# Moving two of eight convolution blocks behind the first attention, and one block off GpSimd

## The chip, the cores and the metric

One core of a Trainium2 chip runs the whole program. The metric is the device time of one execution in microseconds (us); several executions are timed and their median is given. The engines are called as in the profile: PE is TensorE (matrix products), DVE is VectorE, ACT is ScalarE, POOL is GpSimd, SP issues the DMA transfers.

## The reference, cut to what matters

The program is a transformer block of a convolution branch, an attention branch and a feed-forward part, followed by two more attention layers. Sequence length is 512, model width 1024, batch 1, all in float32. The change touches the first block alone:

```python
h = rms_norm(x, norm1_g[l])
z = h @ w_in[l]
glu_in, q, k, v, gate_logits = jnp.split(z, SPLITS, axis=-1)
a_val, a_gate = jnp.split(glu_in, 2, axis=-1)
a = a_val * jax.nn.sigmoid(a_gate)
a = causal_depthwise_conv(a, conv_w[l], conv_b[l])      # 1024 channels, 31 taps each
a = jax.nn.silu(rms_norm(a, conv_norm_g[l]))            # the norm sums over all 1024 channels
y_a = a @ w_conv_out[l]
...                                                     # attention of 16 heads on q, k, v -> o
y_b = o @ w_attn_out[l]
g_a, g_b = jnp.split(jax.nn.sigmoid(gate_logits + gate_b[l]), 2, axis=-1)
x = x + (g_a * y_a + g_b * y_b) @ w_out[l]
```

The depthwise convolution needs only `a`, so it can run at any time between the first input products and the norm behind it. That norm needs all 1024 channels.

## The kernel before

All activations lie with channels on the 128 partitions and the 512 positions along the row, so 1024 channels are eight blocks c = 0 to 7. Each float32 product is made of three matmuls on split operands (high part times high part, lines 301 to 303). A step of a product over 128 input channels is called a chunk here: three matmuls of 512 columns. One output block of 128 channels is eight chunks. The weights of a block are loaded by SP into `wraw` (two buffers), copied to `whi` by ACT (line 119), and the rest `wlo` is made by POOL (line 123); a `wraw` buffer is free for the next transfer only when POOL has made its `wlo`.

PE's order is written out by hand: products go into a list (`pe`), and `pe.pull(n)` emits n chunks. After every chunk a function `beside` can emit other work. The bank of PSUM that a product is written to comes from two banks (`pj`), or from four (`pj` and `s`) where `banks["wide"]` is set. Inside the stage "glu" the orders of PE, DVE, ACT and POOL are those of the code. From the first attention on only PE's is; the planner orders the other engines, by the place in the code and by when it expects an operand.

The stages around the change, in the order of the code:

1. "glu", first half: for each c the products of gate and value (16 products, 128 chunks); line 883 on DVE makes `a` of block c and appends the block to a waiting list. From the ninth chunk on, `beside` emits convolution taps: each chunk earns `PACES` credits, 1.03 taps for DVE and 0.26 for POOL.
2. "glu", second half: eight products of the gates of the first branch (64 chunks), taps still beside them.
3. "loop1": 44 chunks (`LEAD[0]`) of q, k and v for the first two pairs of heads with their norms (lines 918 to 932), taps now at 0.6 and 0.24 per chunk; then `taps("dve", 1000)` emits what is left of DVE's taps; then the attention over eight pairs of heads with further products between its steps. Its transposes go to the three PSUM banks `pt` (line 593), from which ACT and DVE take them (lines 595 and 596).
4. "mid1": five gate products (40 chunks), the sum of squares over the convolved blocks (lines 1010 to 1014), the products with `w_attn_out` (64 chunks). After `YB` = 28 of these 64 chunks PE sums over the channels (`pn`), ACT makes `rc` of it, and DVE and ACT make the operands `aS` of `w_conv_out` from the eight blocks (lines 1036 to 1042). Then come the products with `w_conv_out`, block 0 and 1 side by side. Line 1022 on DVE empties the bank of each `w_attn_out` product.

A block of the convolution is 30 taps and a first multiplication (line 824, ACT). On DVE a tap is one instruction (line 831) that adds into a `pt` bank, which ACT copies out at the end (line 833). Two blocks (three towards the end of one) are taken in turn, so that neighbouring taps belong to different blocks where two are there. On POOL (blocks 1 and 3, `ON_POOL`) a tap is two instructions: ACT multiplies into one of four buffers (line 836), POOL adds (line 837). So DVE has 6 x 30 = 180 taps and POOL 2 x 30 = 60.

Of the kernel before, what the change touches and what calls it, by code (L numbers as in the profile page):

```python
# [32 lines left out]
LN_EPS = 1e-5  # L33
OFF = (0, 128, 384, 768)
LEAD = (44, 34, 38)
ON_POOL = (1, 3)
PACES = {"dve": (1.03, 0.6), "pool": (0.26, 0.24)}
YB = 28
PIECES = 4
GATES3 = ((3, 3), (3, 3), (3, 4), (4, 5), (5, 5), (5, 6), (6, 6), (6, 8))  # L40
P6 = (1, 1, 1, 0, 1, 1, 0, 0, 1, 0)
# [107 lines left out]
def model_kernel(ctx: ExitStack, tc: tile.TileContext, x, norm1_g, w_in, gate_b, conv_w, conv_b, conv_norm_g,  # L149
# [21 lines left out]
    def ps_t():  # L171
        return ps("pt", 3)
# [17 lines left out]
    def act(o, i, func, **kw):  # L190

        ins = nc.scalar.activation(o, i, func, **kw).ins  # L192
        if ordered["load"] is not None and hT:
            tc.add_manual_dep(ins, ordered["load"].name, no_sync)
        ordered["since"].append(ins)

    def act_tables(name):
        ordered["load"], since = None, ordered["since"] or ordered["before"]
        ordered["since"], ordered["before"] = [], since
        if name is not None:  # L200
            ordered["load"] = nc.scalar.preload_act_table_set(name).ins
            for ins in since:
                tc.add_manual_dep(ordered["load"], ins.name, no_sync)
# [191 lines left out]
    def kept():  # L395
        return keep.tile([128, S], F32, name="S8", bufs=ND)
# [26 lines left out]
    with tc.tile_pool(name="rows", bufs=1) as rows, tc.manual_schedule(engines={  # L423
# [21 lines left out]
        for r in range(2):  # L445
            a = slice(64 * r, 64 * r + 64)
# [35 lines left out]
    def columns():  # L482
        p = ps_t()
        for c in range(ND):
            nc.tensor.transpose(p[:, CW * c:CW * c + CW], cr[c // 4][:, 128 * (c % 4):128 * (c % 4) + 128], ident[:CW, :CW])
        nc.vector.tensor_scalar(cw.rearrange("p a b -> p (a b)"), p[:, :ND * CW], 0.5, None, op0=OP.mult)
        p = ps_t()
        nc.tensor.transpose(p[:, :NV], vr, ident[:NV, :NV])
        nc.vector.tensor_copy(vec, p[:, :NV])
        nc.vector.tensor_scalar(gate_half, vec[:, 0:16], 0.5, None, op0=OP.mult)  # L490
        nc.vector.tensor_scalar(cg_half, vec[:, 24:32], 0.5, None, op0=OP.mult)
        nc.vector.tensor_scalar(qg8, vec[:, 56:57], 0.125, None, op0=OP.mult)
        p = ps_t()
        for j in range(2):
            nc.tensor.transpose(p[:, 88 * j:88 * j + 88], fr[:, j, :], ident[:88, :88])
        pv = p[:, :176].rearrange("p (a b) -> p a b", a=4)
        nc.vector.tensor_copy(fw[:, :, :NF], pv[:, :, :NF])
        nc.vector.tensor_scalar(fw[:, :, NF:], pv[:, :, NF:], 0.5, None, op0=OP.mult)

    def tmp(pool):  # L500
        return pool.tile([128, S], F32, name="tmp", bufs={"dsa": 5, "loop1": 5, "loop3": 2, "glu": 3}[pool.name])
# [284 lines left out]
    with tc.tile_pool(name="mix1", bufs=1) as mix1:  # L786
# [20 lines left out]

        o32 = mix1.tile([128, ND, S], F32, name="o32")
        accs, tga = [], {}
        waiting = {"dve": [], "pool": []}  # L810
        lanes = {"dve": [], "pool": []}
        credit = {"dve": 0.0, "pool": 0.0}
        pace = {}
# [25 lines left out]
        def taps(who, n):  # L839

            on, wait = lanes[who], waiting[who]
            while n >= 1:
                while wait and (len(on) < 2 or (len(on) == 2 and min(t.left for t in on) < 4)):
                    on.append(Conv(*wait.pop(0)))
                if not on:
                    break
                t = on.pop(0)
                t.tap()
                if t.left:
                    on.insert(min(1, len(on)), t)  # L850
                n -= 1
            return n
# [11 lines left out]
        def gate_a(c, t):  # L864
            return Product(w_in, 0, 8, 5120 + 128 * c, hT, gate_done(c, t))

        with tc.tile_pool(name="glu", bufs=1) as gp, tc.manual_schedule(engines={
                mybir.EngineType.PE, mybir.EngineType.DVE, mybir.EngineType.Activation, mybir.EngineType.Pool}):
            act_tables("exp_and_others")
            banks["wide"] = True  # L870

            def glu(c):
                t = tmp(gp)

                def gate(p):
                    act(t, p, AF.Tanh, scale=0.5)

                def val(p):
                    def out():
                        accs.append(kept())  # L880
                        on_pool = c in ON_POOL
                        a = o32[:, ND - 1 - ON_POOL.index(c), :] if on_pool else accs[c]
                        nc.vector.scalar_tensor_tensor(a, t, 1.0, p, op0=OP.add, op1=OP.mult)
                        credit["dve"] -= 1
                        waiting["pool" if on_pool else "dve"].append((c, a))
                    pe.after(3, out)

                return (Product(w_in, 0, 8, 1024 + 128 * c, hT, gate), Product(w_in, 0, 8, 128 * c, hT, val))

            for c in range(ND):  # L890
                for pr in glu(c):
                    pe.skewed(pr)
                if c == 0:
                    pe.pull(8)
                    columns()
                    pace.update({who: p[0] for who, p in PACES.items()})
                    pe.beside = beside
                pe.pull(len(pe.todo))
            for c in range(ND):
                t = mix1.tile([128, S], F32, name="tg", bufs=ND - 1) if c < ND - 1 else rc2  # L900
                pe.skewed(gate_a(c, t))
                pe.pull(len(pe.todo))
            pe.finish()
            pace.update({who: p[1] for who, p in PACES.items()})

# [89 lines left out]
        act_tables(None)  # L995
        with tc.tile_pool(name="mid1", bufs=1) as mp:
            banks["wide"] = True
            oS = []
            for c in range(ND):
                h, l = act_pair(mp, "C", ND)  # L1000
# [19 lines left out]
            def yb_done(c):  # L1020
                t = tga[ND + c]
                return lambda p: nc.vector.scalar_tensor_tensor(t, t, 1.0, p, op0=OP.add, op1=OP.mult)

            for c in range(ND):
                pe.add(w_attn_out, 0, 8, 128 * c, oS, yb_done(c))
            pe.pull(YB)
            pn = ps_t()
# [138 lines left out]
    gs, og, waiting = {}, [], {}  # L1166
# [419 lines left out]
```

## Time and profile before

| | us |
|---|---|
| timed runs, median of 3 (lowest to highest) | 1601.13 (1597.56 to 1601.93) |
| the profiled execution, timed | 1601.03 |
| its span in the profile | 1598.9 |

In the profile PE is busy 1527.2 us of the span, DVE 1121.4, ACT 845.4, POOL 806.5. The granted clock of PE is given as a share of its upper level, 2.4 GHz; the lower level, 1.2 GHz, is 0.5. Times in the text are from the span's start. A row of a timeline gives start and length in us, and in brackets how long the engine stood idle before it and whose work ended that.

### The profile page before, as it was taken

What the parts mean: (1) busy time and instruction counts of PE and PEld (TensorE: products, weight loads), DVE (VectorE), ACT (ScalarE), POOL (GpSimd) and SP (SyncE); (2) the same over time, 40 slices, a digit from 0 to 9 for tenths busy, and PEclk for the clock granted to TensorE, in tenths of its full rate; (3) what the DMA queues carried; (4) which work ended last, traced back from release to release, by engine and by line L of the source; (5) the groups of instructions that cost most, each with busy time, mean ns of one, the idle gap of its engine ahead of it and who ended that gap; (6) DMA issues with size and microseconds to landing.
All of it is one profiled execution on the core that took longest, in us unless ns stands there. A gap on an engine that the chain in (4) does not pass through costs nothing.

```text
span 1598.9 us, 21378 instructions
## 1 busy us (share of the span) xinstructions
PE 1527.2 (96%) x7870; PEld 1296.7 (81%) x7870; DVE 1121.4 (70%) x1837; ACT 845.4 (53%) x1524; POOL 806.5 (50%) x680
## 2 busy tenths in 40 slices
PE   7999799998999999999999999999999789999996
PEld 6877688887878888888888887888887678888885
DVE  8998777776166467727735669988887765777764
ACT  4455787777552444424333444366766345666652
POOL 3789944332744653454444474445442875334324
PEclk9999899999999999999999999999999899999998
DMA  4323212221233423343333242322220313212212
GB/s 149 88 87 98 86 54 73 60 67 40 67 105 105 126 86 92 93 118 91 90 110 89 84 125 66 80 80 66 67 67 14 92 40 106 67 54 80 67 52 80
DMA packets 234604, 130.37 MB, mean 82 GB/s; under 512 B 5206, under 2 KB 232774, under 8 KB 234500
## 3 DMA queue, kind: packets, MB, share of 16 engines
q1 hardware_dynamic: 234356, 128.75, 27.7%
q8 instruction: 62, 1.02, 0.3%
q14 instruction: 42, 0.34, 0.1%
q10 hardware_dynamic: 144, 0.26, 0.0%
HBM read 126.90 MB, written 2.10 MB: 81 GB/s over the span
## 4 chain that ended last, share of the span: by engine, by line
PE 57%; DVE 23%; ACT 7%; POOL 5%; issue 5%; DMA 2%; DVEq 0%; SPq 0%; ACTq 0%; POOLq 0%
PE pj L301 10%; PE pj L302 9%; PE pj L303 9%; PE s L302 5%; PE s L303 5%; PE s L301 5%; DVE pt L831 5%; PE o L512 2%; POOL wlo L123 2%; PE pt L593 2%; PE pj L325 2%; PE pj L327 2%; PE pj L326 2%; POOL S L837 2%; DVE score L1442 1%
## 5 line engine op out<-in xcount | busy, mean ns | idle before, releaser
L123 POOL TENSOR_TENSOR wlo<-wraw,whi 128x256 fp32r<-128x256 f32 (+2 forms) x548 | 653.8, 1218 | 684.4 <-ACT whi L119 639.0
L301 PE MATMUL pj<-Ah,whi 128*128 128x512 f32 (+3 forms) x896 | 362.2, 404 | 15.2 <-DVE v L718 9.8
L119 ACT CAST whi<-wraw 128x1024 fp32r<-128x1024 f32 (+3 forms) x255 | 243.8, 965 | 224.3 <-PE pj L302 82.1
L303 PE MATMUL pj<-Ah,wlo 128*128 128x512 f32 (+3 forms) x896 | 350.4, 391 | 2.5 <-POOL wlo L123 2.5
L302 PE MATMUL pj<-Al,whi 128*128 128x512 f32 (+3 forms) x896 | 350.7, 391 | 0.0
L301 PEld LDWEIGHTS pj<-Ah,whi 128*128 128x128 f32 (+1 forms) x896 | 171.2, 191 | 41.9 <-issue 9.1
L303 PEld LDWEIGHTS pj<-Ah,wlo 128*128 128x128 f32 (+1 forms) x896 | 170.3, 190 | 39.1 <-POOL wlo L123 3.4
L302 PEld LDWEIGHTS pj<-Al,whi 128*128 128x128 f32 (+1 forms) x896 | 171.1, 191 | 24.4
L301 PE MATMUL s<-Ah,whi 128*128 128x512 f32 (+1 forms) x352 | 135.8, 386 | 4.0 <-ACT Ah L1298 4.0
L302 PE MATMUL s<-Al,whi 128*128 128x512 f32 (+1 forms) x352 | 135.7, 386 | 3.6 <-DVE Al L1299 3.6
L303 PE MATMUL s<-Ah,wlo 128*128 128x512 f32 (+1 forms) x352 | 135.6, 385 | 1.0 <-POOL wlo L123 1.0
L831 DVE SCALAR_TENSOR_TENSOR pt<-S,cw,pt 128x496 f32<-128x496 f32 (+19 forms) x180 | 124.8, 738 | 6.4 <-ACT pt L824 3.8
L325 PE MATMUL pj<-whi,Ah 128*128 128x256 f32 x384 | 112.4, 293 | 1.4 <-DVE q L533 1.4
L596 DVE TENSOR_TENSOR PTl<-pt,PTh 128x512 fp32r<-128x512 f32 x144 | 86.0, 598 | 32.9 <-ACT PTh L595 31.9
L327 PE MATMUL pj<-whi,Al 128*128 128x256 f32 x384 | 108.4, 282 | 0.0
L326 PE MATMUL pj<-wlo,Ah 128*128 128x256 f32 x384 | 108.3, 282 | 0.0
L192 ACT ACTIVATE P<-P,nm 128x128 f32<-128x128 f32 (+3 forms) x128 | 72.0, 563 | 63.2 <-DVE nm L626 61.9
L744 DVE SCALAR_TENSOR_TENSOR u<-ur,fw,u 128x511 f32<-128x511 f32 x44 | 74.9, 1705 | 37.5 <-ACT u L743 37.5
L837 POOL TENSOR_TENSOR S<-S,o 128x511 f32<-128x511 f32 (+29 forms) x60 | 78.2, 1317 | 15.4 <-ACT o L836 14.3
L595 ACT CAST PTh<-pt 128x512 fp32r<-128x512 f32 x144 | 73.1, 513 | 19.6 <-PE pt L593 19.1
L302 PEld LDWEIGHTS s<-Al,whi 128*128 128x128 f32 x352 | 67.8, 193 | 17.1 <-DVE Al L1299 4.5
L301 PEld LDWEIGHTS s<-Ah,whi 128*128 128x128 f32 x352 | 67.9, 193 | 17.1 <-ACT Ah L1298 4.6
(334 smaller groups left out, 3250.8 us busy)
## 6 DMA issues: line engine op xcount, KB each, us to landing
wraw<-in_w_in_dram SPq DMA_DIRECT2D x56, 512.0 KB
wraw<-in_w_up_dram SPq DMA_DIRECT2D x44, 512.0 KB
wraw<-in_w_in_a_dram SPq DMA_DIRECT2D x36, 512.0 KB
wraw<-in_w_in_b_dram SPq DMA_DIRECT2D x32, 512.0 KB
wraw<-in_w_down_dram SPq DMA_DIRECT2D x16, 512.0 KB
wraw<-in_w_attn_out_dram SPq DMA_DIRECT2D x8, 512.0 KB
wraw<-in_w_conv_out_dram SPq DMA_DIRECT2D x8, 512.0 KB
wraw<-in_w_out_dram SPq DMA_DIRECT2D x8, 512.0 KB
```

The lines of the kernel that those rows point to most:

```text
L119: nc.scalar.copy(h, s)
L123: nc.gpsimd.tensor_sub(l[:, k], s[:, k], h[:, k].bitcast(F32))
L301: nc.tensor.matmul(o, hv[:, k, :], ah, start=first, stop=False)
L302: nc.tensor.matmul(o, hv[:, k, :], al, start=False, stop=False)
L303: nc.tensor.matmul(o, lv[:, k, :], ah, start=False, stop=last)
L325: nc.tensor.matmul(o, ah, hv, start=k == 0, stop=False)
L326: nc.tensor.matmul(o, ah, lv, start=False, stop=False)
L327: nc.tensor.matmul(o, al, hv, start=False, stop=k == 7)
L596: nc.vector.tensor_sub(l[:, :at], pt[:, :at], f32(h)[:, :at])
L744: nc.vector.scalar_tensor_tensor(u[:, 1:], v[:, :S - 1], fw[:, 1, j:j + 1], u[:, 1:], op0=OP.mult, op1=OP.add)
L831: nc.vector.scalar_tensor_tensor(o, a, w, o, op0=OP.mult, op1=OP.add)
L837: nc.gpsimd.tensor_add(o, o, t)
```

## The change

Of the blocks 1 and 3 only block 1 stays on POOL; block 3 goes to DVE. Blocks 6 and 7 leave the waiting list of "glu" for a list of their own, and their 60 taps are emitted at the head of "mid1", before anything else of that stage. The credit of POOL falls from 0.26 and 0.24 to 0.2 and 0.2. `YB` goes from 28 to 34.

```diff
-ON_POOL = (1, 3)
-PACES = {"dve": (1.03, 0.6), "pool": (0.26, 0.24)}
-YB = 28
+ON_POOL = (1,)
+LATE = (6, 7)
+PACES = {"dve": (1.03, 0.6), "pool": (0.2, 0.2)}
+YB = 34
@@
-        waiting = {"dve": [], "pool": []}
+        waiting = {"dve": [], "pool": [], "late": []}
@@
-                        waiting["pool" if on_pool else "dve"].append((c, a))
+                        waiting["pool" if on_pool else "late" if c in LATE else "dve"].append((c, a))
@@
         with tc.tile_pool(name="mid1", bufs=1) as mp:
             banks["wide"] = True
+            waiting["dve"] += waiting["late"]
+            taps("dve", 1000)
```

## Rows read from the trace of the kernel before

**Rows 1.** The page, part 1: busy us, share of the span, instructions, by engine.

```profile
PE 1527.2 (96%) x7870; PEld 1296.7 (81%) x7870; DVE 1121.4 (70%) x1837; ACT 845.4 (53%) x1524; POOL 806.5 (50%) x680
```

**Rows 2.** Busy us of each engine by stage: stretch, its length, engines, clock, DMA.

```profile
20.00:120.00 100.00, 96.85 (x425) 79.16 (x424) 92.47 (x136) 47.08 (x65) 75.02 (x44) 0.98 0.33 95
120.00:153.00 33.00, 32.64 (x145) 26.68 (x144) 33.00 (x53) 18.16 (x26) 32.75 (x24) 1.00 0.36 104
153.00:206.00 53.00, 40.28 (x208) 34.28 (x207) 34.23 (x43) 35.49 (x58) 48.44 (x32) 0.90 0.29 85
206.00:403.00 197.00, 190.65 (x1116) 164.98 (x1115) 146.07 (x304) 153.68 (x328) 71.60 (x83) 0.98 0.20 58
403.00:455.00 52.00, 52.00 (x225) 42.94 (x225) 7.54 (x8) 25.62 (x37) 35.88 (x21) 0.97 0.30 87
455.00:480.00 25.00, 22.63 (x93) 18.21 (x93) 23.32 (x28) 13.14 (x22) 10.30 (x4) 0.93 0.29 84
```

**Rows 3.** PE's waits from 95 to 206 us: us in total, times, longest.

```profile
PE pj L301 <- DVE v L718: 8.1, 2, 7.2
PE pj L301 <- ACT tmp L929: 4.6, 1, 4.6
PE pj L303 <- POOL wlo L123: 2.5, 2, 2.2
```

**Rows 4.** Timeline of PE, behind its two long stalls.

```profile
163.39 0.65 PE L301 MATMUL pj<-Ah,whi 128*128 128x512 f32 x1 [4.61 <-ACT tmp L929]
...
166.82 0.48 PE L303 MATMUL pj<-Ah,wlo 128*128 128x512 f32 x1
...
196.94 0.77 PE L301 MATMUL pj<-Ah,whi 128*128 128x512 f32 x1 [7.23 <-DVE v L718]
...
200.91 0.49 PE L301 MATMUL pj<-Ah,whi 128*128 128x512 f32 x1
```

**Rows 5.** Timeline of POOL, ahead of the two long stalls.

```profile
155.28 4.72 POOL L123 TENSOR_TENSOR wlo<-wraw,whi 128x1024 fp32r<-128x1024 f32 x2
...
180.54 10.01 POOL L837 TENSOR_TENSOR S<-S,o 128x483 f32<-128x483 f32 x7
```

**Rows 6.** Timeline of ACT, where its queue stood.

```profile
97.47 0.78 ACT L824 ACTIVATE pt<-S,vec,cw 128x512 f32<-128x512 f32 x1 [7.22 <-DVE S L883]
...
161.31 1.04 ACT L119 CAST whi<-wraw 128x1024 fp32r<-128x1024 f32 x1 [4.24 <-DMA wraw<-in_w_in_dram]
...
183.90 1.89 ACT L836 ACTIVATE o<-o,cw 128x482 f32<-128x482 f32 x3 [3.87 <-POOL S L837]
```

**Rows 7.** Timeline of DVE: taps of one block, of two blocks; late key operands.

```profile
34.11 12.49 DVE L831 SCALAR_TENSOR_TENSOR pt<-S,cw,pt 128x511 f32<-128x511 f32 x16 [1.88 <-ACT pt L824]
...
118.78 21.92 DVE L831 SCALAR_TENSOR_TENSOR pt<-S,cw,pt 128x496 f32<-128x496 f32 x34
...
194.06 2.27 DVE L560 TENSOR_TENSOR kl<-tmp,k 64x512 fp32r<-64x512 f32 x1
```

**Rows 8.** Timeline of PE behind the attention.

```profile
403.10 0.63 PE L301 MATMUL pj<-Ah,whi 128*128 128x512 f32 x1
...
472.78 0.47 PE L301 MATMUL pj<-Ch,whi 128*128 128x512 f32 x1 [2.37 <-ACT th L192]
```

**Rows 9.** Timeline of ACT (452.44) and DVE behind the attention.

```profile
452.44 0.69 ACT L192 ACTIVATE rc<-pt,eps 128x512 f32<-128x512 f32 x1
...
427.35 0.69 DVE L1017 TENSOR_TENSOR stl<-ssum,sth 128x512 fp32r<-128x512 f32 x1 [0.69 <-ACT sth L1016]
...
455.11 5.54 DVE L1036 SCALAR_TENSOR_TENSOR S<-S,cg_half,rc 128x512 f32<-128x512 f32 x5 [6.22 <-ACT rc L192]
...
471.96 0.67 DVE L1022 SCALAR_TENSOR_TENSOR tga<-tga,pj 128x512 f32<-128x512 f32 x1
```

**Rows 10.** The page, part 5: what empties a bank of the attention's transposes.

```profile
L596 DVE TENSOR_TENSOR PTl<-pt,PTh 128x512 fp32r<-128x512 f32 x144 | 86.0, 598 | 32.9 <-ACT PTh L595 31.9
...
L595 ACT CAST PTh<-pt 128x512 fp32r<-128x512 f32 x144 | 73.1, 513 | 19.6 <-PE pt L593 19.1
```

## The prediction, made before the changed kernel was run

> **What bounds the kernel now.** The first view is busy time by engine: PE is busy 1527.2 of 1598.9 us [rows 1], so everything that a change of order can win is PE's idle time and the time it runs at the lower clock. The second is the same by stage [rows 2]. From 206 to 403 us (attention) PE lacks 6.4 us of 197, from 403 to 455 nothing. From 153 to 206 (the head of the attention) it lacks 12.7 us of 53 at a granted clock of 0.90, while POOL is busy 48.4 of 53. In the stretch before, 120 to 153, DVE is busy 33.00 of 33 and POOL 32.75. The reader is to see that PE starves just where the convolution's taps fill POOL and DVE.
>
> The third view names the waits: 15.2 us from 95 to 206 us, in three groups of 8.1, 4.6 and 2.5 [rows 3]. The timelines tell what stood behind each.
>
> - 4.6 us up to 163.39 [rows 4]: PE wants a bank that ACT has not emptied. ACT's queue stood at 161.31, 4.24 us, on a weight copy whose transfer had not landed [rows 6]. That transfer needs a `wraw` buffer, which is free when POOL has made `wlo`; POOL did two of these in a row from 155.28 to 160.0 [rows 5], late, because taps stood ahead of them.
> - 7.23 us up to 196.94 [rows 4]: POOL ran seven taps from 180.54 to 190.6 [rows 5], ACT stood 3.87 us at 183.90 on a tap's first half whose buffer POOL still held [rows 6], and the norm of the keys waited in ACT's queue behind it. DVE made the keys' lower parts at 194.06 only, at 2.27 us for 64x512 [rows 7], and emptied the bank behind them.
> - 2.5 us on `wlo` itself. ACT's queue stood 7.22 us at 97.47 on block 5, whose `a` DVE had not made yet [rows 6]; POOL's taps and splits queue behind ACT's.
>
> **Part 1: less in the first stages.** The credits, stepped chunk by chunk through the 192 chunks of the first two stages, emit 170 of DVE's 180 taps and 42 of POOL's 60 there before; the rest goes beside the head of the attention, up to chunk 267 on POOL. Changed, DVE's 150 taps are out at chunk 172 and POOL's 30 at chunk 179: no tap is left beside the attention.
>
> POOL's load per product of eight chunks: PE needs 8 x 3 x 0.231 = 5.5 us (0.231 is 52.00 us over 225 matmuls [rows 2]); POOL needs one `wlo`, 4.72 / 2 = 2.36 us, and 8 x 0.26 = 2.1 taps at 10.01 / 7 = 1.43 us [rows 5], 5.3 us in all. Changed, 1.6 taps make it 4.6 us: there is slack for the first time. ACT loses 30 multiplications, which are the instructions at which its queue stands.
>
> DVE gets block 3 in place of 6 and 7. Its rate is the same per chunk, so the question is whether it keeps up. A tap costs 12.49 / 16 = 0.78 us where one block is alone and 21.92 / 34 = 0.645 where two take turns [rows 7]. Before, blocks 0, 2 and 4 ran alone for a time; changed, there are always two from chunk 68 on. In 16 chunks (11.1 us) DVE then has 15.5 taps and line 883, 15.5 x 0.645 + 0.7 = 10.7 us. It keeps up, closely.
>
> Worth: 15.2 us of waits. Behind the two long stalls PE also ran slowly: 8 matmuls from 163.39 to 166.82 at 0.43 us and 9 from 196.94 to 200.91 at 0.44 [rows 4], against 0.231, which is 8 x 0.20 + 9 x 0.21 = 3.5 us at the lower of the two clock levels (1.2 GHz). Together 18.7 us. The bounds are 0 (every wait finds another cause) and 18.7. I take 17.2, leaving 1.5 us, as ACT will still stand at block 3 as it did at block 5 [rows 6], with POOL now ready to absorb it.
>
> **Part 2: 60 taps behind the attention.** DVE is nearly free there: 7.54 us busy from 403 to 455 [rows 2]. Two blocks take turns, so 60 x 0.645 = 38.7 us. From 403.1, where PE begins the gates [rows 8], and with at most the 7.5 us of other work in between, the taps end between 442 and 449. The two first multiplications on ACT lie in front of them, and each block takes one of three `pt` banks, which the attention's last transposes give back at that time. Behind the taps come copy, square, sum, cast and subtraction, five steps of about 0.7 us (the last is 0.69 [rows 9]); with a second square and sum I take 5 us, so the operands of the channel sum are there at 447 to 454.
>
> PE comes to that sum six chunks later than before, 6 x 3 x 0.231 = 4.2 us. `rc` began at 452.44 [rows 9], so the sum was done by then; it moves to about 456.6. The taps are hidden by 2 to 9 us. If that cover goes, each us costs one. Queued behind the taps on DVE is line 1022, which empties the banks of the `w_attn_out` products: four banks and 5.5 us per product give the first of them until about 453, so it can wait for the taps' end.
>
> The shift of 4.2 us hits the chain from `rc` to `aS`, which starts at 455.11 and would start at 459.3. Before, the eighth `w_attn_out` product waited 2.37 us [rows 8] for the bank of the fourth, emptied at 471.96, 16.9 us into that chain [rows 9]. With `YB` at 34 the fourth product (chunk 32) is over before the sum, so its line 1022 stands ahead of the chain and this stall goes. What is late next is the fifth: at the same place in the chain it is emptied at 459.3 + 16.9 + 0.7 = 476.9. The `w_attn_out` products would end at 472.78 - 2.37 + 5.5 = 475.9, and the first `w_conv_out` product wants that bank: 1 us, and its neighbour, which wants the sixth product's bank, somewhat more. Against the 2.37 us won, the bounds are -2.4 (no new stall) and +4.2 (the whole shift is felt). I take +1, nearer to the row of the old stall than to the whole shift, since 64 - 34 = 30 chunks (20.8 us) still cover most of a chain of some 22 us.
>
> **The sum.** Against the profiled execution, 1601.03 us (its span and 2.1 us around it; 0.1 from the median of the runs): 1601.03 - 17.2 + 1.0 = 1584.8, so 1585. The best corner is 1601.0 - 18.7 - 2.4 = 1580.
>
> **The rivals.**
>
> - *Half of the front gain.* The 8.1 us group is the norm's own length and not POOL's doing: PE reaches the scores before the keys are ready in any case. Then 8.1 + 1.9 us stay: 1585 + 10 - 1.5 = 1593. For it: four engines take part in that chain. Against: POOL's seven taps and ACT's 3.87 us lie right on it. Chance 0.13.
> - *The sum of squares is late.* The Trainium skill (VectorE: DVE Perf Modes, The DRAIN you can't avoid) says that a DVE instruction does not start until the one before has left the pipeline, so that taking turns would win nothing. The rows say 0.645 against 0.78 us, and the sum goes by them. As a mechanism of this kernel: at 0.78 us, the rate of one block alone, 60 taps take 46.8 us and end at 450 to 457, the operands come at 455 to 462 and PE waits 0 to 6 us at the sum: 1585 to 1591. It decides from taps that end behind 451. Chance 0.07.
> - *The late blocks start too early; slower.* The planner may take up the two blocks as soon as a `pt` bank and ACT are free, inside the attention: their inputs have long been there. They would hold two of the three banks while 38.7 us of taps pass through the 51 us that DVE has free from 206 to 403 [rows 2], about three quarters of that stretch. Each of the 48 transposed groups (144 in three attentions [rows 10]) then finds one bank and waits up to the 0.51 + 0.60 us of the cast and subtraction that empty it [rows 10]: 36 x 0.55 to 36 x 1.1 = 20 to 40 us, against 16 won: 1605 to 1625, and slower from 0.45 us a group on. Against: three groups follow each other closely and leave no bank free for long. Chance 0.09.
> - *It does not do what it says.* PE's waits move: transfers of weights, not POOL, set the pace (ACT's 4.24 us [rows 6] is put down to a transfer), or ACT's stand at block 3 brings the `wlo` wait back. Then little is left: 1597 to 1603. Chance 0.09.
>
> **How the numbers follow.** My forecast, 1579 to 1592, has 0.62. Faster by over 0.3% (about what a measurement of this kernel can tell from no change) means under 1596.3: the forecast, the late sum and nearly all of the half gain, 0.80. Within 0.3%: the last rival and the edges of its neighbours, 0.11. Slower: 0.09. The range 1579 to 1598 leaves out the slow rival and most of the last one, under 2 in 10.
>
> **What would show it.** Right: PE's waits on lines 718, 929 and 123 before the attention fall from 15.2 us to under 3; the clock there is back near 1.0; the last POOL tap lies before PE's first q product; DVE shows 60 taps from about 403 to 445 and none between; no wait on `pn`; a stall of 1 to 4 us where `w_conv_out` begins. Wrong: taps on DVE inside the attention with waits at line 593; a wait at the channel sum; a `wlo` or bank wait of over 4 us left before 200 us.

## The result and the profile after

| | us |
|---|---|
| before, median | 1601.51 |
| changed, median of 4 (lowest to highest) | 1582.52 (1581.45 to 1584.24) |
| ratio, 95% interval | 0.9888 (0.987 to 0.9906) |
| changed, the profiled execution: timed; span | 1582.75; 1580.9 |

The change takes 19 us. Lines of the changed kernel carry numbers one higher than before up to the head of "mid1" (832 is the tap on DVE, 838 the tap on POOL, 124 `wlo`, 719 the bank of v), and three higher behind it (1025 empties the `w_attn_out` banks, 1039 to 1045 make `aS`).

Busy time by stage, in the columns of [rows 2]: stretch, its length, PE, its weight loads, DVE, ACT, POOL, clock, DMA.

```profile
20.00:120.00 100.00, 98.45 (x439) 80.78 (x438) 94.63 (x144) 45.21 (x63) 72.69 (x42) 1.00 0.35 101
120.00:150.00 30.00, 30.00 (x133) 24.60 (x132) 25.50 (x37) 11.61 (x17) 21.64 (x16) 1.00 0.30 88
150.00:190.00 40.00, 38.74 (x217) 33.73 (x217) 17.23 (x25) 25.15 (x42) 25.41 (x17) 1.00 0.40 119
190.00:387.00 197.00, 190.81 (x1117) 165.16 (x1116) 146.54 (x307) 153.69 (x326) 67.28 (x79) 0.98 0.20 60
387.00:440.00 53.00, 52.58 (x231) 42.94 (x230) 42.55 (x65) 26.04 (x37) 38.04 (x22) 1.00 0.32 94
440.00:465.00 25.00, 21.21 (x83) 16.66 (x83) 23.37 (x28) 13.57 (x20) 11.83 (x4) 0.89 0.26 76
```

The head of the attention, 53 us before, is where the time went: PE now lacks 1.3 us of 40 there at the full clock, and POOL has 25 us of work in 40 where it had 48 in 53. The attention itself is as it was. Some 35 us of new work on DVE appear from 387 to 440, beside a PE that is 52.6 us busy of 53. In the last stretch PE lacks 3.8 us at a clock of 0.89, more than before.

PE's waits from 95 to 190 us, against [rows 3]:

```profile
PE pj L304 <- POOL wlo L124: 0.9, 1, 0.9
PE pj L302 <- DVE v L719: 0.4, 1, 0.4
```

And from 200 to 465 us, the longest:

```profile
PE s L302 <- ACT th L193: 3.6, 1, 3.6
PE o L513 <- ACT PTh L596: 1.7, 1, 1.7
```

POOL, where before seven taps stood in a row [rows 5]:

```profile
147.35 1.24 POOL L838 TENSOR_TENSOR S<-S,o 128x483 f32<-128x483 f32 x1 [5.74 <-ACT o L837]
148.55 2.39 POOL L124 TENSOR_TENSOR wlo<-wraw,whi 128x1024 fp32r<-128x1024 f32 x1
150.89 1.22 POOL L838 TENSOR_TENSOR S<-S,o 128x482 f32<-128x482 f32 x1
...
155.80 2.39 POOL L124 TENSOR_TENSOR wlo<-wraw,whi 128x1024 fp32r<-128x1024 f32 x1 [1.33 <-ACT whi L120]
```

The last tap is done at 152.1. ACT stood 29.8 us in 16 places for POOL's taps before, and nowhere for them now; POOL waits for ACT instead. Behind the attention, DVE's timeline with PE's at the channel sum (435.02) and at the first `w_conv_out` product (459.92):

```profile
382.19 1.54 DVE L832 SCALAR_TENSOR_TENSOR pt<-S,cw,pt 128x511 f32<-128x511 f32 x2 [0.52 <-ACT pt L825]
...
386.67 36.65 DVE L832 SCALAR_TENSOR_TENSOR pt<-S,cw,pt 128x510 f32<-128x510 f32 x57
...
431.24 2.70 DVE L1017 TENSOR_TENSOR ssum<-ssum,th 128x512 f32<-128x512 f32 x2 [2.12 <-ACT th L1016]
...
434.62 0.69 DVE L1020 TENSOR_TENSOR stl<-ssum,sth 128x512 fp32r<-128x512 f32 x1 [0.69 <-ACT sth L1019]
...
439.52 3.40 DVE L1039 SCALAR_TENSOR_TENSOR S<-S,cg_half,rc 128x512 f32<-128x512 f32 x5 [3.61 <-ACT rc L193]
...
459.10 0.68 DVE L1025 SCALAR_TENSOR_TENSOR tga<-tga,s 128x512 f32<-128x512 f32 x1
...
383.50 0.63 PE L302 MATMUL pj<-Ah,whi 128*128 128x512 f32 x1
...
435.02 0.40 PE L1031 MATMUL pt<-sth,ones_d 128*128 128x512 f32 x1
...
459.92 0.77 PE L302 MATMUL s<-Ah,whi 128*128 128x512 f32 x1 [3.61 <-ACT th L193]
...
466.47 0.39 PE L304 MATMUL s<-Ah,wlo 128*128 128x512 f32 x1
```

Between the last tap and the sum, ACT's queue:

```profile
426.12 1.05 ACT L120 CAST whi<-wraw 128x1024 fp32r<-128x1024 f32 x1 [3.62 <-DMA wraw<-in_w_attn_out_dram]
427.07 0.58 ACT L834 COPY S<-pt 128x512 f32<-128x512 f32 x1
429.07 1.05 ACT L120 CAST whi<-wraw 128x1024 fp32r<-128x1024 f32 x1 [1.41 <-DMA wraw<-in_w_attn_out_dram]
430.02 0.58 ACT L834 COPY S<-pt 128x512 f32<-128x512 f32 x1
430.50 1.16 ACT L1016 ACTIVATE th<-S 128x512 f32<-128x512 f32 x2
```

The 60 taps follow each other at 36.65 / 57 = 0.643 us, the operand of the channel sum is there just as PE asks for it, and the bank that `w_conv_out` needs is emptied at 459.8, 20 us into the chain that starts at 439.52. The 15 matmuls from 459.92 to 466.47 take 0.43 us each instead of 0.231.

### The profile page after: what moved, and what is told of

Same layout as the page of the kernel before. It is cut to its first block, busy times and chain, and to the rows that moved or that the text cites. A ratio compares the mean times of both kernels' runs of the same rounds, so it can differ in the third digit from the quotient of the medians.

```text
span 1580.9 us, 21344 instructions
## 1 busy us (share of the span) xinstructions
PE 1519.2 (96%) x7870; PEld 1290.7 (82%) x7870; DVE 1133.5 (72%) x1867; ACT 827.1 (52%) x1495; POOL 767.0 (49%) x650
## 4 chain that ended last, share of the span: by engine, by line
PE 57%; DVE 25%; ACT 8%; issue 4%; POOL 3%; DMA 3%; SPq 0%; DVEq 0%; ACTq 0%; POOLq 0%
PE pj L302 9%; PE pj L303 9%; PE pj L304 9%; DVE pt L832 6%; PE s L303 5%; PE s L302 5%; PE s L304 5%; PE o L513 3%; POOL wlo L124 2%; PE pt L594 2%; PE pj L326 2%; PE pj L328 2%; PE pj L327 2%; PE s L583 1%; DVE score L1445 1%
## 5 line engine op out<-in xcount | busy, mean ns | idle before, releaser
L832 DVE SCALAR_TENSOR_TENSOR pt<-S,cw,pt 128x494 f32<-128x494 f32 (+26 forms) x210 | 141.8, 733 | 5.5 <-ACT pt L825 3.5
L596 ACT CAST PTh<-pt 128x512 fp32r<-128x512 f32 x144 | 73.1, 513 | 19.1 <-PE pt L594 18.7
L594 PE MATMUL pt<-ident,P 128*128 128x128 f32 x480 | 76.7, 273 | 2.5 <-ACT P L193 0.9
```

The lines of the kernel that those rows point to most:

```text
L594: nc.tensor.transpose(pt[:, at:at + 128], self.P[r][:, k0:k0 + 128], ident)
L832: nc.vector.scalar_tensor_tensor(o, a, w, o, op0=OP.mult, op1=OP.add)
```

## The experiments

Each is the changed kernel with the edit shown; e1 to e10 are their numbers. The times to compare with are 1582.5 us (changed) and the kernel before of the same session, 1599.5 to 1601.3 us.

**Which half of the change wins (e1, e2).** First the late blocks alone, with two blocks on POOL as before:

```diff
-ON_POOL = (1,)
-PACES = {"dve": (1.03, 0.6), "pool": (0.2, 0.2)}
+ON_POOL = (1, 3)
+PACES = {"dve": (1.03, 0.6), "pool": (0.26, 0.24)}
```

> Changed kernel, but with blocks 1 and 3 back on GpSimd at the old credits (0.26, 0.24); blocks 6 and 7 stay late, YB 34. VectorE's taps in front fall from 180 to 120, GpSimd's stay 60 with some 20 of them beside the head of the attention. Theory (GpSimd's queue, through ScalarE's, makes the two long stalls): most of the 15.2 us of waits stay, 8 to 15 us of them, and 3 us of slow matmuls; with 1 us lost behind the attention: 1593 to 1602 us. Rival (VectorE's load makes them): the waits of lines 718 and 929 vanish and only the 2.5 us on wlo are left: 1584 to 1588 us.

Measured: 1605.18 us, ratio to before 1.0027 (1.0017 to 1.0037): slower, 3 us above the 1593 to 1602 that was expected, on the side of the theory. PE's waits from 95 to 206 us:

```profile
PE pj L302 <- ACT rc L193: 6.5, 1, 6.5
PE pj L302 <- DVE v L719: 3.5, 1, 3.5
PE pj L326 <- ACT tmp L930: 3.2, 1, 3.2
PE pj L304 <- POOL wlo L124: 2.1, 1, 2.1
```

That is 15.3 us, as much as before [rows 3], although DVE has 60 taps less there and has done its last at 132 us. POOL still runs its taps in rows between the splits, and ACT stands behind them. One piece of each queue:

```profile
180.10 8.14 POOL L838 TENSOR_TENSOR S<-S,o 128x490 f32<-128x490 f32 x6
...
181.38 0.70 ACT L837 ACTIVATE o<-o,cw 128x486 f32<-128x486 f32 x1 [2.85 <-POOL S L838]
```

So 60 taps less on DVE take nothing off the waits: they move, and their sum stays. The first scores of the attention begin at 205.7 us, 4.0 later than before. Behind the attention the same stall of 3.6 us stands as in the changed kernel, and from the first gate product to the end of the `w_conv_out` products it takes 123.3 us against 120.4 before. The late blocks alone win nothing in front and lose 3 us behind. The attention between was 3.2 us shorter, and why stays open.

Then the other half alone, one block on POOL, none late:

```diff
-LATE = (6, 7)
-YB = 34
+LATE = ()
+YB = 28
```

> Changed kernel with no late block (LATE empty, YB 28): block 3 on VectorE, blocks 6 and 7 in front too, 210 taps on VectorE. By the credits 171 are out at the end of the gates, 26 go beside the 44 chunks of the attention's head and 13 in one go behind them. Theory (GpSimd's queue): the stall up to 163.39 us (4.6) and the wlo waits (2.5) vanish, and of the 8.1 us some comes back, since 39 taps (25 us) now stand in VectorE's queue among the norms of the first heads: 1588 to 1597 us. Rival (only the count of taps in front matters, on whichever engine): 30 taps less on GpSimd and 30 more on VectorE win nothing: 1599 to 1606 us.

Measured: 1588.22 us, ratio 0.9922 (0.9906 to 0.9938), inside the theory's range at its lower end. PE's waits from 95 to 215 us:

```profile
PE pj L302 <- ACT tmp L930: 2.6, 1, 2.6
PE pt L594 <- ACT P L193: 2.5, 1, 2.5
PE pj L302 <- DVE v L719: 2.1, 2, 1.3
PE s L580 <- DVE nm L627: 1.4, 2, 0.8
```

No `wlo` wait is left in this stretch, and the two long ones are cut to 2.6 and 1.3 us. What remains is DVE's doing: its taps go on until 205.9 us, between the norms and the first scores, and the attention ends at 392.4 us and not at 383.5. The block taken off POOL wins 13 of the 19 us alone. The late blocks are worth some 5 us more (the intervals of 0.9922 and 0.9888 just touch; the two profiled spans are 4.4 us apart), and only together with it: they make room on DVE for what POOL gives away. Taking the block off POOL also takes 30 multiplications of 0.7 us off ACT; no run separates the two.

**The credit (e8).** The changed kernel with POOL's old credit for its one block:

```diff
-PACES = {"dve": (1.03, 0.6), "pool": (0.2, 0.2)}
+PACES = {"dve": (1.03, 0.6), "pool": (0.26, 0.24)}
```

> Changed kernel with GpSimd's old credits of 0.26 and 0.24 per chunk for its one block. Theory (what counted is that GpSimd's taps end inside the first stages and that one block alone does not fill it): the 30 taps end some 35 chunks earlier, at about chunk 150; the load while they run rises to about 5.0 of 5.5 us a product; 0 to 2 us slower than the changed kernel, 1582 to 1585 us. Rival (the lower credit made the gain): the waits on wlo come back, 2 to 5 us of them: 1585 to 1588 us.

Measured: 1583.5 us, ratio 0.9889 (0.9872 to 0.9905). No difference that can be told; the credit of a single block is free.

**When PE asks for the channel sum (e3).** `YB` back at 28:

```diff
-YB = 34
+YB = 28
```

> Changed kernel with YB back at 28. TensorE asks for the channel sum some 4.2 us earlier, at about 432.6 us; the taps end at 423.3 and the sum's operand is there at 435.3 as before. Theory (cover nearly used up): a new wait of 2 to 3 us at the sum, the chain behind it starts about 1.5 us earlier and the stall before the first w_conv_out products changes by 1 to 2 us either way: 1581 to 1586 us, so within 0.3% of the changed kernel. Rival (YB 34 only costs, the taps are hidden at 28 too): no wait at the sum, and 2 to 4 us faster than the changed kernel: 1578 to 1581 us.

Measured: 1580.53 us, ratio 0.9877 (0.9861 to 0.9893): the theory's wait is there, a little longer than the 2 to 3 us expected. The time lies 0.5 us below the theory's range, among the rival's times, whose mechanism (no wait) did not come; by the intervals it is no different from the changed kernel. PE at the sum:

```profile
432.07 0.50 PE L1031 MATMUL pt<-sth,ones_d 128*128 128x512 f32 x1 [3.46 <-ACT sth L1019]
```

PE pays 3.5 us here and is spared the 3.6 us before `w_conv_out`. The bank does not come back earlier: it is emptied 76.2 us behind the first gate product, and 76.3 in the changed kernel. It is PE that comes later, 78.5 us behind that product where it stood ready at 72.8, since it waited at the sum and ran slowly behind it. Between 28 and 34 the change only chooses where PE waits.

**What the stall before w_conv_out is (e4, e10).** The first two products get banks that are free there:

```diff
-            prods = [Product(w_conv_out, 0, 8, 128 * c, aS, ya_done(c)) for c in range(ND)]
+            prods = [Product(w_conv_out, 0, 8, 128 * c, aS, ya_done(c), bank={"p": ps_t()} if c < 2 else None) for c in range(ND)]
```

> Changed kernel in which the first two w_conv_out products write to two of the three pt banks, which are free there, and no longer wait for the banks of the fifth and sixth w_attn_out products. Theory (that stall of 3.61 us at 459.92 and the 13 or so slow matmuls behind it are the wait for a bank): both go, and the operands aS are there in time: 4 to 6 us less than the changed kernel, 1577 to 1579 us. Rival (the operands themselves are late, the bank is only named last): 0 to 2 us less, 1581 to 1583 us, with waits on lines 1044 and 1045 instead.

Measured: 1576.42 us, ratio 0.9843 (0.9829 to 0.9858), 0.6 us better than the theory's range. PE's timeline at the first of the two products, where the stall stood:

```profile
456.10 0.39 PE L302 MATMUL pt<-Ah,whi 128*128 128x512 f32 x1
```

The busy time of two stretches, in the columns of [rows 2]:

```profile
440.00:456.00 16.00, 16.00 (x72) 13.27 (x71) 16.00 (x20) 10.74 (x16) 6.91 (x3) 1.00 0.29 87
456.00:465.00 9.00, 9.00 (x42) 7.44 (x41) 7.38 (x9) 2.84 (x4) 4.96 (x2) 1.00 0.20 58
```

PE is busy throughout at the full clock: the operands `aS` were in time and the bank alone was late. The gain is the stall and the slow matmuls behind it, 3.6 + 15 x 0.2 = 6.6 us. The kernel ran once more, on one chip with e9:

> The kernel of e4 once more (pt banks, YB 34), beside e9 on one chip, since the two are to be compared. Theory (no wait of TensorE is left behind the attention in it): 1575 to 1578 us, no slower than e9. Rival (its lead over YB 28 was the session's): 1579 to 1583 us.

Measured: 1575.03 us, ratio 0.9848 (0.9831 to 0.9864). The ratio is that of e4, so the lead was not the session's; e9 took 1584.62 us beside it. It is the fastest of all and beats both kernels of this document.

**Both together (e7).** With the banks free, `YB` at 28:

> Changed kernel with the pt banks for the first two w_conv_out products, and YB at 28. Theory (with the bank wait gone, the only effect of YB is when TensorE asks for the sum): the 3.5 us wait at the sum that YB 28 showed is now bare, 1578 to 1581 us, slower than the same kernel at YB 34 (1576.4) by 2 to 4 us. Rival (YB 28 was better by itself, as its median was 2 us under that of the changed kernel): 1572 to 1575 us.

Measured: 1580.91 us, ratio 0.9877 (0.9863 to 0.9892), inside the theory's range, and 4.5 us slower than e4 where 2 to 4 were expected. The wait of 3.5 us at the sum is now bare, and slow matmuls stand behind it. `YB` at 34 is right once nothing else waits behind it.

**Why the sum's operand comes late (e9).** In that kernel the taps end at 421.4 and the operand comes 12 us later. DVE instead of ACT copies the late blocks out:

```diff
-                    if j == 0:
+                    if j == 0 and self.c in LATE:
+                        nc.vector.tensor_copy(self.a, self.acc)
+                    elif j == 0:
                         pe.after(2, lambda: nc.scalar.copy(self.a, self.acc))
```

> The kernel of e7 (pt banks, YB 28), in which VectorE and not ScalarE copies the two late blocks out of their banks, right behind their last tap. In e7 the taps end at 421.4 us and the sum's operand comes at 433.4, 12 us later; ScalarE's two copies stand in its queue behind weight copies that wait for transfers (3.77 us at 424.33, 1.33 at 427.19). Theory (the place of these copies in ScalarE's queue makes most of the 12 us): the operand comes 3 to 6 us earlier, the wait of 3.5 us at the sum falls under 1 us: 1576 to 1578.5 us. Rival (the squares that follow stand in the same queue behind the same transfers): the wait stays over 2.5 us, 1580 to 1582 us.

Measured: 1584.62 us, ratio 0.9898 (0.9883 to 0.9913). The theory fell: the copies were done at 424.9, yet PE's wait stayed, at 3.9 us. The rival's mechanism came, at a time 2.6 us above its range. ACT's queue in that kernel:

```profile
426.97 1.05 ACT L120 CAST whi<-wraw 128x1024 fp32r<-128x1024 f32 x1 [3.99 <-DMA wraw<-in_w_attn_out_dram]
429.63 1.05 ACT L120 CAST whi<-wraw 128x1024 fp32r<-128x1024 f32 x1 [1.61 <-DMA wraw<-in_w_attn_out_dram]
430.58 1.15 ACT L1018 ACTIVATE th<-S 128x512 f32<-128x512 f32 x2
```

The squares come next in ACT's queue behind the same two weight copies, which wait for transfers, so moving one step of the chain off ACT does nothing. That these copies make the delay is read from the timeline; no run took them away. The profiled execution is 3.7 us longer than that of e7, but 2.0 of them lie in the attention, which the edit does not touch and which took 201.2 us in e4 and 199.1 in e10, the same kernel; 1.1 lie behind it.

**When the cover is gone (e5).** Three late blocks:

```diff
-LATE = (6, 7)
+LATE = (5, 6, 7)
```

> Changed kernel with three late blocks (5, 6 and 7) in place of two: 90 taps behind the attention, 120 in front. Theory (the cover behind the attention is used up by two blocks): in the changed kernel the taps run from 382.2 to 423.3 us and the sum's operand follows 12 us later, 1.5 us ahead of TensorE; 30 taps more at 0.643 us are 19 us, so TensorE waits some 17 us at the channel sum. In front nothing is left to win, since the waits there are 2.8 us in all: 1595 to 1601 us. Rival (the front still gains from fewer taps, or the sum's chain has slack): 1580 to 1590 us.

Measured: 1600.5 us, ratio 0.9997 (0.9987 to 1.0008). The whole gain is given back at one place:

```profile
456.23 0.80 PE L1031 MATMUL pt<-sth,ones_d 128*128 128x512 f32 x1 [23.23 <-ACT sth L1019]
```

The wait is 23 us where 17 were expected. The third block runs alone for most of its taps:

```profile
431.15 0.69 DVE L1017 TENSOR_TENSOR ssum<-ssum,th 128x512 f32<-128x512 f32 x1 [6.89 <-POOL ssum L1017]
...
434.26 19.26 DVE L832 SCALAR_TENSOR_TENSOR pt<-S,cw,pt 128x506 f32<-128x506 f32 x25
```

19.26 / 25 = 0.77 us each, and ahead of it DVE stood 6.9 us behind POOL's part of the sum of squares. One late block more costs about what its 30 taps last, 18 us over the changed kernel.

**The slow rival, made by hand (e6).** The two late blocks ahead of the attention's loop:

```diff
             pe.pull(LEAD[0])
+            waiting["dve"] += waiting["late"]
             taps("dve", 1000)
@@
-            waiting["dve"] += waiting["late"]
-            taps("dve", 1000)
```

> Changed kernel in which the two late blocks are emitted ahead of the attention's loop (behind the 44 chunks of its head) and not behind it: the case that the slow rival of the prediction feared, made on purpose. They hold two of the three pt banks until their 60 taps are through. Rival's price: 36 groups of transposes that wait 0.55 to 1.1 us each, or the head's norms stand behind 38.7 us of taps; in both cases 20 to 40 us more than the changed kernel: 1602 to 1622 us. Against it (VectorE's 51 free us in the attention take the taps without harm, and the stage behind the attention becomes shorter): 1578 to 1585 us.

Measured: 1616.21 us, ratio 1.0096 (1.0079 to 1.0112), 34 us over the changed kernel and inside the price named. The mechanism is not the one of the rival, though. PE's waits from 20 to 490 us, the longest:

```profile
PE s L580 <- DVE nm L627: 28.3, 2, 27.8
PE pj L302 <- DVE v L719: 3.4, 1, 3.4
```

It is one wait of 27.8 us: the taps stand in DVE's queue ahead of the attention's first maxima. Not one wait at line 594, where the transposes want a `pt` bank, is longer than 1 us. The rival's own case, taps that hold the banks between the attention's steps, was thus not made.

## Why the prediction was right, point by point

**What bounds the front.** Right, and the runs separate what the trace could only suggest: with 60 taps fewer on DVE the 15.2 us stay (e1), with one block off POOL the long waits shrink to 2.6 and 1.3 us (e2). That the block on POOL starts them is shown. Whether POOL's additions or ACT's multiplications for it weigh more is not, and the path through ACT's queue is argued from the timelines. In the stall up to 196.94 there was a second path that the prediction did not name; the last section has it. Of the signs named beforehand one failed: POOL's last tap ran from 150.89 to 152.1, behind PE's first q product (146.78). The one `wlo` wait that is left, 0.9 us up to 150.99, is of that kind: a tap stood ahead of the split.

**The front's worth.** 17.2 us were taken of 18.7, and 18.9 measured, at the first scores of the attention, before and after:

```profile
201.71 0.22 PE L579 MATMUL s<-k,q 128*128 128x128 f32 x1
...
182.78 0.22 PE L580 MATMUL s<-k,q 128*128 128x128 f32 x1
```

The waits from 95 us on fell by 14.0, from 15.2 to 1.3, and the slow matmuls behind the two long stalls account for 3.5. Of the 1.4 us left over 0.5 are there by 38 us, ahead of POOL's first tap at 48.7, and are not tied to the change; the others are mostly slow matmuls behind the shorter stalls, which the prediction left out. The reason given for keeping 1.5 us back did not hold: ACT stood at block 3 as forecast, 8.91 us up to 72.93, and PE had no wait from there to 150 us.

**DVE keeps up.** It did no harm, but kept up less well than forecast. A tap takes 0.643 us with two blocks against the 0.645 used. The last front taps, due by chunk 172, which PE ends at 133.2 us, were done at 146.0: DVE was 12.8 us behind. PE's first q product came at 146.78, 20 chunks behind chunk 172, and that was room enough. The rival that hung on the taps' rate did not come: 0.77 us alone and 0.643 in turns, here too. The Trainium skill (VectorE: DVE Perf Modes, The DRAIN you can't avoid) states the rule that a DVE instruction does not start until the one before has left the pipeline, and adds that a next one that is not held starts earlier. The plain rule does not describe these taps.

**The cover behind the attention.** This is the term that was mis-sized. The taps end at 423.3, 39.8 us after the gates begin, as forecast (39 to 46). From there to the sum's operand 5 us were taken and 12 measured. The prediction counted five steps at the length of one instruction; it did not count what stands in ACT's queue between them, two weight copies with transfers that are not there yet, and a sum at 2.70 us for two in place of 1.4. It also took the start of `rc` for the time at which PE asks; PE had asked 1.7 us earlier:

```profile
450.73 0.39 PE L1028 MATMUL pt<-sth,ones_d 128*128 128x512 f32 x1
```

The cover was put at 2 to 9 us and was nil: PE came at 435.02, and the operand's second half was done at 435.3. It held because the taps ended at the early bound, and that was luck: at the late bound, 7 us on, PE would have waited about 7 us, by the same rows.

**The chain to w_conv_out.** The place was right, the size too small. The chain began 4.0 us later in its stage (56.0 us behind the first gate product against 52.0), 4.2 forecast. The fourth product's stall went, and the fifth was late next, both as forecast. Its bank was emptied 20.2 us into the chain, not 17.6, so PE stood 3.61 us and 0.18 more, against 2.37 before: 1.4 us more, where 1 was taken. The slow matmuls behind these stalls were left out in this part, though the front's were counted: 15 x 0.2 = 3.0 us behind the new one, 8 x 0.2 = 1.6 behind the old. That the bank makes the stall is shown by e4, which takes stall and slow matmuls away and wins 6 us. From the first gate product to the end of the `w_conv_out` products, where the next transposes begin, it is 120.4 us before and 123.4 after, 3.0 more and inside the bounds of -2.4 and 4.2:

```profile
523.48 1.03 PE L1070 MATMUL pt<-ident,xr 128*128 128x128 f32 x8
...
506.87 1.03 PE L1073 MATMUL pt<-ident,xr 128*128 128x128 f32 x8
```

**The sum.** 1601.0 - 18.9 (front) - 0.7 (the attention, 201.4 to 200.7 us long) + 3.0 (behind it) - 1.4 (all that follows) = 1583.0 against 1582.75 timed and 1585 forecast. The front gave 1.7 us more than taken and the back cost 2.0 more, and the two nearly cancel: that is luck. The attention and the rest are not touched by the change; their 2.1 us are of the size by which e4 and e10, one kernel, differ in the attention alone.

**The rivals.** Half of the front gain: no, 0.4 us are left of the wait behind the norm, so its length is no bound. The late sum: not in the changed kernel, but it was nearer than its chance of 0.07 said, as e3 and e5 show. The early start: the planner did not do it; the taps put ahead of the attention by hand cost 34 us, by DVE's queue and not by the banks. Transfers that set the pace in place of POOL: no, the long waits went with POOL's block.

## What to carry to other kernels

An engine that splits weights for PE and also carries spare work can set PE's pace through the buffers it gives back late; taking work off it paid here although its busy share of the whole run was 50%, and the waits showed up under other engines' names. Moving work behind a later stage is worth what it makes room for: alone it lost 4 us here. Where a moved chain shares an in-order queue with transfers, count what stands in that queue between its steps, and add the slow matmuls behind each new stall of PE.

## What the runs showed of the hardware that was not expected

DVE's taps cost the same with and without POOL at work: in the changed kernel's run of taps behind the attention, 27 taps beside a running POOL instruction follow each other at 0.642 us and 7 beside none at 0.637. A sum on DVE does not: in e9 the same instruction took 2.36 us while POOL made a `wlo` (430.76 to 433.13) and 0.68 without.

```profile
431.32 2.36 DVE L1019 TENSOR_TENSOR ssum<-ssum,th 128x512 f32<-128x512 f32 x1 [5.83 <-ACT th L1018]
...
434.19 0.68 DVE L1019 TENSOR_TENSOR ssum<-ssum,th 128x512 f32<-128x512 f32 x1
```

The Trainium skill (SBUF: State Buffer, Who interferes with whom) says that a DVE instruction with two inputs in SBUF contends with a GpSimd instruction that reads SBUF, and that one with at most one SBUF input, outside DVE's 2-port modes, does not. The trace agrees with both halves: a tap reads one operand from SBUF and adds to a PSUM bank, the sum reads two from SBUF.

The same stands in the long stall of the kernel before. The two subtractions that make the keys' lower parts read two SBUF operands and took 2.42 us (at 190.97) and 2.27 us (at 194.06 [rows 7]), where the median of that instruction is 0.69. Each lay beside a `wlo`, the second beside this one:

```profile
193.44 2.34 POOL L123 TENSOR_TENSOR wlo<-wraw,whi 128x1024 fp32r<-128x1024 f32 x1 [0.59 <-ACT whi L119]
```

That is some 3 us of the chain ahead of that stall by a path that does not lead through ACT's queue. For a choice of what to put beside POOL's work, the number of SBUF operands counted more here than the engine's busy share.
